# A decoder layer's sample attention: steps of four batches in place of steps of two

## The chip, the cores and the metric

The kernel runs on one core of one Trainium2 chip. Its time is the device time of one execution in microseconds (us); of several executions the median stands. The profile is one further execution, taken by the hardware profiler. In its rows PE is TensorE's matrix multiplication and PEld its loading of weights; DVE is VectorE, ACT is ScalarE, POOL is GpSimd and SP is SyncE, whose queue issues most of the transfers (SPq). A matrix product of f32 data appears as two records, so that a run of eight products is shown as x16.

## The reference, cut to what matters

One layer of a decoder is computed for two groups of requests that share the weights: a prompt of 1024 positions, and a sample group of 8 batches with 8 new positions each and 4096 cached ones. The change is in the attention of the sample group. It has 8 query heads of 64 channels in two groups of 4, and each group has one key and value head. Three branches are added with gates: the attention over compressed blocks of the cache, the attention over selected blocks of 64 cached positions, and a window of 512.

```python
def cmp_attention(q, k_cmp, v_cmp, q_pos):
    ...
    s = jnp.einsum('btgrd,bcgd->bgrtc', q, k_cmp).astype(jnp.float32) * ATTN_SCALE
    p = masked_softmax(s, mask)
    o = jnp.einsum('bgrtc,bcgd->btgrd', p.astype(v_cmp.dtype), v_cmp)
...
def slc_block_attention(q_b, idx_b, ok_b, pos_b, k_blocks, v_blocks):
    ...
    s = jnp.einsum('btgrd,bgtkpd->bgrtkp', q_b, k_sel).astype(jnp.float32) * ATTN_SCALE
    ...
    return jnp.einsum('bgrtkp,bgtkpd->btgrd', p.astype(v_sel.dtype), v_sel)
...
def window_sample(q, kw_ext, vw_ext, pos0):
    ...
    return window_attention(q[:, None], kw_ext[:, None], vw_ext[:, None], q_pos, k_pos)[:, 0]
```

Here b is the batch, t the position, g the group, r the head within the group, d the channel. A batch and a group have r x t = 4 x 8 = 32 query rows. The kernel doesn't gather the selected blocks: it computes the scores of all cached positions and masks those that were not selected.

## The kernel before, in words

The kernel is one Python class that writes the instructions of the whole layer. Its `run` is a planner: tasks are generators, and at each turn the one with the lowest priority number that is ready by the planner's clock goes on. The clock adds up costs written in the code (`mm`, `use`); for an f32 product with at most 64 weight columns `mm` counts 0.55 of the full cost, with at most 32 columns 0.27, and never fewer than 128 moving columns. The order in which the planner writes the instructions is the base of the order on each engine; a scheduler with a timeline of its own may still move them. `tc.issue_after(x)` makes the instructions written in its block come after x on x's engine.

After the input projection comes the stage with attention, in which three tasks share the engines. `prompt_attention` works through 32 units (8 query blocks, 2 halves of the heads, 2 branches), with priority 1.8 + `v_done`/32. `compress` makes the compressed keys and values of the sample batches 3 to 7 (0 to 2 are done earlier) from cache pages, which pass through three `stream` tiles. `sample_attention` has priority 2 + 1.1 x `u_done`/36. When the stage is over the kernel goes on to the output projection, whose weights and inputs are loaded by SP.

**The sample attention before.** The batches are taken in four pairs p; a pair has 9 units, 8 of 512 cached positions for each of the two batches and one for the window, 36 units in all. The queries stand in `qb` with 64 columns for a batch: 32 for each group, and zeros in the 64 channel rows of the other group. So the product of `qb` (128 rows, 64 columns) with the keys of 512 positions gives the 64 query rows of a batch, and the two batches of a pair fill the 128 partitions of a bank of PSUM, each in its own half of TensorE's columns. One unit is then:

1. two score products of 512 columns into a bank `S` (L135, `bank<-unit,qb` or `bank<-stream,qb`; the keys and values of a unit come in a tile `unit` or `stream`);
2. the mask and the row minimum on DVE (L1264, L1267), the exponential on ACT (L1271), both into `e`;
3. four transposes on PE (L139, `bank<-ident,e`) and the copy to `spt` (L150 on ACT or L152 on DVE);
4. eight value products of 128 columns (L135, `bank<-unit,spt` or `bank<-stream,spt`: 4 tiles of positions, 2 batches), each with both groups' values, of which a query row needs one half;
5. the copy of the sum to `part`.

A unit's tile is filled by 8 gathers of 128 KB from `cacheB` (L517) or by one load of the window (L1232). Two tiles `unit` are there from the start; the three `stream` tiles join once all batches are compressed (`cmp_done == 8`, in `sample_load`). A unit is written when the one before the last is done (`u_done >= u - 1`).

`sample_select` comes ahead of a pair. It waits for the pair's two compressed batches, computes the compressed branch (products named `bank<-kvc,qb` and `bank<-kvc,ct`), the new positions (`bank<-kn,qb`, `bank<-vt,ct`), the choice of blocks (`bias`) and the gates (`gr`). `sample_combine` joins the 12 parts of a pair on DVE (`co`, L1319 and L1321) and stores them to `mix_d` through SP (L1332), where the output projection reads them.

Other products that the text names: `bank<-wada,sc` (L135) has 32 weight columns and four column tiles side by side, `bank<-vt,c_w` has weights of 64 rows and 64 columns in four tiles, two row halves by two column halves; `bank<-pt,vt` are the value products of the prompt, and `bank<-kh,qs` its scores.

Of the kernel before, what the change touches and what calls it, by code (L numbers as in the profile page):

```python
# [17 lines left out]
P = 128  # L18
# [42 lines left out]
class Kernel:  # L61
# [181 lines left out]
    def constants3(self, c):  # L243
        nc = self.nc
        with self.pool("ctmp") as tp:
# [47 lines left out]
            a = tp.tile([P, 4, 64], F32, name="a")  # L293
            for b2 in range(2):
                nc.gpsimd.iota(a[64 * b2:64 * b2 + 64], pattern=[[-16, 4], [1, 64]], base=-8 * b2,
                               channel_multiplier=0, allow_small_or_imprecise_dtypes=True)
            ge = tp.tile([P, 4, 64], F32, name="ge")
            nc.vector.tensor_scalar(ge, a, 0.0, None, op0=OP.is_ge)
            ok = tp.tile([P, 4, 64], F32, name="ok")
            nc.vector.scalar_tensor_tensor(ok, a, tv[:, 0:1], ge, op0=OP.is_le, op1=OP.mult)  # L300
            self.m_new = c.tile([P, 4, 64], F32, name="m_new")
# [10 lines left out]
            self.sel = c.tile([P, 4, P], F32, name="sel")  # L312
            si = tp.tile([P, 4, 2, 8, 8], F32, name="si")
            for p in range(4):
                nc.gpsimd.iota(si[:, p], pattern=[[-8, 2], [0, 8], [-1, 8]], base=-64 - 16 * p,
                               channel_multiplier=1, allow_small_or_imprecise_dtypes=True)
            nc.vector.tensor_scalar(self.sel.rearrange("a p r -> a (p r)"), si.rearrange("a p b g t -> a (p b g t)"),
# [3 lines left out]
            hi = tp.tile([P, 8], F32, name="hi")  # L321
            for b2 in range(2):
                nc.gpsimd.iota(hi[64 * b2:64 * b2 + 64], pattern=[[-8, 8]], base=0, channel_multiplier=1,
                               allow_small_or_imprecise_dtypes=True)
            hg = tp.tile([P, 8], F32, name="hg")
            nc.vector.tensor_scalar(hg, hi, 0.0, None, op0=OP.is_ge)
            self.hind = c.tile([P, 8], F32, name="hind")
            nc.vector.scalar_tensor_tensor(self.hind, hi, 7.0, hg, op0=OP.is_le, op1=OP.mult)

# [773 lines left out]

    def sample_setup(self, pool):
        nc = self.nc
        self.qb = pool.tile([P, NB, 64], F32, name="qb")
        nc.vector.memset(self.qb, 0.0)
        for g in range(2):
            s = slice(64 * g, 64 * g + 64)
            nc.vector.tensor_copy(  # L1110
                self.qb[s].rearrange("p b (g r t) -> p g b r t", g=2, r=4)[:, g],
                self.q[s, :, SEQ:].rearrange("p r (b t) -> p b r t", t=NT))
        self.kn = pool.tile([P, 2, 64], F32, name="kn")
        nc.vector.tensor_copy(self.kn, self.ksw[:, :, SEQ:])
        self.use("dve", 1.5)

    def rows(self, b2):
        return slice(64 * b2, 64 * b2 + 64)

    def sample_select(self, pool, p, st):  # L1120

        nc = self.nc
        part = pool.tile([P, 12, P], F32, name="part", bufs=2)
        nm = pool.tile([P, 12], F32, name="nm", bufs=2)
        den = pool.tile([P, 12], F32, name="den", bufs=2)
        st.update(part=part, nm=nm, den=den)
        kv = []
        yield from self.hold(lambda: self.cmp_done >= 2 * p + 2)
        for b2 in range(2):
            t = pool.tile([P, 2, 256], F32, name="kvc", bufs=2)  # L1130
            nc.sync.dma_start(t, self.cmp_d[2 * p + b2])
            kv.append(t)
        yield self.use("dma", 1.5, self.t["pe"]) + 2.5
        S = yield from self.bank_of("S")
        S2 = yield from self.bank_of("S")
        for b2 in range(2):
            self.mm(S[self.rows(b2), 0:256], self.qb[:, 2 * p + b2], kv[b2][:, :, 0:P], True, True)
        for b2 in range(2):
            self.mm(S2[self.rows(b2), 0:128], self.qb[:, 2 * p + b2], self.kn.rearrange("p j t -> p (j t)"), True, True)

# [48 lines left out]
        for h in range(2):  # L1189
            self.tr(tr[:, h * P:(h + 1) * P], pc[:, 1 + h * P:1 + (h + 1) * P])  # L1190
# [985 lines left out]
```

## Time and profile before

| | |
|---|---|
| time, median of 3 runs (lowest to highest) | 1708.9 us (1705.45 to 1711.09) |
| time of the profiled execution | 1706.47 us |
| span of its records | 1704.6 us |
| PE busy | 1609.1 us, 94% of the span |
| DVE busy | 1113.6 us, 65% |
| ACT busy | 817.8 us, 48% |
| POOL busy | 706.9 us, 41% |
| granted TensorE clock over the span | 0.98 of full speed |

The time has 1.9 us outside the span. The busy time of PE counts the modelled ends of products that overlap in the array, so that 94% is not the share of the array's peak. Times in the rows below are counted from the start of the span.

### The profile page before, as it was taken

Reading aid. Unit: us, or ns where it says so; the run is one execution under the profiler, and the core shown is the slowest. Engines: PE = TensorE matmul, PEld = TensorE weight load, DVE = VectorE, ACT = ScalarE, POOL = GpSimd, SP = SyncE. Lnnn points to the kernel's source line nnn. Section 1 sums busy time; section 2 is a strip of 40 time slices with the busy share of each in tenths; the row PEclk is TensorE's granted clock in tenths of the full one; section 3 lists DMA queues with packets and bytes.
Section 4 is the critical chain, followed back from the end, with each engine's and each line's share of the span. In section 5 each row is a group of like instructions: output and inputs, shape, how many; then the busy total and the mean of one; then the engine's idle time right before and its main releaser. Section 6 shows DMA issues by size and latency. Waiting matters only on the chain. (4 is left out here: it accounts for less than half of the span.)

```text
span 1704.6 us, 34455 instructions
## 1 busy us (share of the span) xinstructions
PE 1609.1 (94%) x11961; PEld 1414.5 (83%) x11961; DVE 1113.6 (65%) x2830; ACT 817.8 (48%) x1878; POOL 706.9 (41%) x814
## 2 busy tenths in 40 slices
PE   6999999998998999999899789999999999889998
PEld 2999997887776566666699779999999998889997
DVE  4603326686665766866699986555555556988877
ACT  3512215245766776766675643332333334555554
POOL 3101110013331322222106476445555555898976
PEclk9899999998999999999999989999999999999999
DMA  9555564226654644432783223225222225744423
GB/s 341 170 179 177 162 208 143 80 63 196 196 171 125 199 138 146 143 92 83 233 244 90 92 72 117 96 97 191 97 100 96 96 97 187 240 128 132 131 82 122
DMA packets 177120, 245.08 MB, mean 144 GB/s; under 512 B 25889, under 2 KB 132578, under 8 KB 176626
## 3 DMA queue, kind: packets, MB, share of 16 engines
q1 hardware_dynamic: 157090, 215.37, 40.4%
q0 software_dynamic: 5840, 16.10, 2.9%
q10 hardware_dynamic: 14016, 11.41, 2.2%
q8 instruction: 95, 1.56, 0.4%
q14 instruction: 79, 0.65, 0.1%
HBM read 202.33 MB, written 44.67 MB: 145 GB/s over the span
## 5 line engine op out<-in xcount | busy, mean ns | idle before, releaser
L135 PE MATMUL bank<-b_hi,w_hi 128*128 128x272 f32 x1232 | 352.3, 292 | 9.2 <-DVE f_v L1551 4.5
L135 PE MATMUL bank<-b_lo,w_hi 128*128 128x272 f32 x1232 | 356.0, 291 | 2.9 <-DVE b_lo L160 2.9
L135 PE MATMUL bank<-b_hi,w_lo 128*128 128x272 f32 x1232 | 352.0, 290 | 1.3 <-DVE w_lo L160 1.3
L135 PEld LDWEIGHTS bank<-b_hi,w_hi 128*128 128x128 f32 x1232 | 232.3, 191 | 12.3 <-ACT b_hi L164 5.1
L135 PEld LDWEIGHTS bank<-b_lo,w_hi 128*128 128x128 f32 x1232 | 234.4, 190 | 4.5 <-DVE b_lo L160 4.4
L135 PEld LDWEIGHTS bank<-b_hi,w_lo 128*128 128x128 f32 x1232 | 233.1, 190 | 2.5 <-DVE w_lo L160 2.3
L160 POOL TENSOR_TENSOR w_s<-w_raw 128x512 f32<-128x512 f32 (+1 forms) x122 | 167.3, 1373 | 149.4 <-DVE w_lo L160 133.0
L1050 POOL TENSOR_SCALAR P<-P,st 128x128 f32<-128x128 f32 (+12 forms) x192 | 112.0, 592 | 259.2 <-DVE st L1048 86.3
L160 DVE TENSOR_TENSOR w_lo<-w_raw,w_hi 128x512 fp32r<-128x512 f32 (+2 forms) x129 | 115.0, 898 | 100.7 <-ACT w_hi L164 85.8
L164 ACT ACTIVATE w_hi<-w_raw 128x512 fp32r<-128x512 f32 (+2 forms) x130 | 86.4, 674 | 150.5 <-PE bank L135 100.5
L160 DVE TENSOR_TENSOR w_lo<-w_s,w_hi 128x512 fp32r<-128x512 f32 (+1 forms) x144 | 130.3, 908 | 43.1 <-ACT w_hi L164 39.2
L160 POOL TENSOR_TENSOR x<-x,d_m 128x272 f32<-128x272 f32 x144 | 140.1, 994 | 22.9 <-DVE x L1745 11.1
L135 PE MATMUL bank<-stream 128*128 128x128 f32 x1056 | 134.1, 285 | 6.8 <-DMA stream<-in_cacheA 6.7
L135 PEld LDWEIGHTS bank<-stream 128*128 128x128 f32 x1056 | 129.0, 200 | 13.8 <-issue 8.7
L164 ACT ACTIVATE w_hi<-w_s 128x512 fp32r<-128x512 f32 (+1 forms) x144 | 89.0, 624 | 102.4 <-PE bank L135 51.5
L135 PE MATMUL bank<-h_hi,w_hi 128*128 128x384 f32 (+1 forms) x384 | 130.9, 341 | 2.4 <-ACT py L865 2.3
L135 PE MATMUL bank<-h_hi,w_lo 128*128 128x384 f32 (+1 forms) x384 | 127.1, 331 | 0.0
L1042 ACT ACTIVATE P<-P,st 128x128 f32<-128x128 f32 (+12 forms) x192 | 113.2, 591 | 28.4 <-DVE st L1033 13.8
L135 PE MATMUL bank<-h_lo,w_hi 128*128 128x384 f32 (+1 forms) x384 | 126.6, 330 | 0.0
L135 PE MATMUL bank<-g_hi,w_hi 128*128 128x272 f32 x308 | 91.8, 300 | 14.5 <-DVE x L1745 8.2
L139 PEld LDWEIGHTS bank<-ident,P 128*128 128x128 f32 (+1 forms) x592 | 63.2, 138 | 50.7 <-issue 33.6
L1033 DVE CUSTOM_DVE_ANT_0 P<-bank,m_slc 128x256 f32<-128x256 f32 (+5 forms) x136 | 68.1, 513 | 54.2 <-PE bank L135 29.2
(368 smaller groups left out, 4114.8 us busy)
## 6 DMA issues: line engine op xcount, KB each, us to landing
wada<-in_wada SPq DMA_DIRECT2D x96, 256.0 KB, 5.3
stream<-in_cacheA SPq DMA_DIRECT2D x192, 128.0 KB, 3.3
w_raw<-in_wup SPq DMA_DIRECT2D x48, 512.0 KB, 4.3
unit<-in_cacheB SPq DMA_DIRECT2D x152, 128.0 KB, 2.3
g_raw<-g_d SPq DMA_DIRECT2D x70, 272.0 KB, 3.1
stream<-in_cacheB SPq DMA_DIRECT2D x104, 128.0 KB, 2.2
w_raw<-in_wout SPq DMA_DIRECT2D x24, 512.0 KB, 4.7
g_d<-f_T SPq DMA_DIRECT2D x84, 136.0 KB, 1.8
```

The source lines that it names most:

```text
L135: return self.nc.tensor.matmul(out, lhsT, rhs, start=start, stop=stop, skip_group_check=chain)
L139: self.nc.tensor.transpose(out, in_, self.ident)
L160: (self.nc.vector if eng == "dve" else self.nc.gpsimd).tensor_tensor(out, a, b, op=op)
L164: self.nc.scalar.activation(hi, src, AF.Copy)
L1033: nc.vector.tensor_tensor_reduce(out=Pt[:, h, col:col + n], in0=S[:, p0:p0 + n], in1=mk, scale=-1.0, scalar=3e38, op0=OP.add, op1=OP.min, ...
L1042: nc.scalar.activation(Ps, Ps, AF.Exp, scale=-1.0, bias=sy[:, 0:1], accum_out=sy[:, 1:2])
L1050: nc.gpsimd.tensor_scalar(Ps, Ps, sy[:, 3:4], 0.0, op0=OP.mult, op1=OP.add)
```

## The change

The 8 batches are taken in two groups Q of four. A query block of `qb` has 32 columns without zeros: the heads and positions of one group, its 64 channels in the group's own half of the rows. A step u (18 in all) holds two of the earlier units, thus four batches, and has two banks `S`, one for each group g, with the four batches in four strips of 32 partitions. Its eight score products have 64 rows, 32 weight columns and 512 moving columns, and each has a tile of the array of its own (2 row halves by 4 column strips). The 32 value products have 128 rows, 32 weight columns and 64 moving columns (2 groups, 4 tiles of positions, 4 batches). DVE, ACT and the transposes have as many instructions for a step as for two units before, except that the sum is copied once for a step. `together` writes the first product and puts the others behind it on PE; the first is one of the last batch's. The two buffers `e` and the two `spt` are now both taken by one step, as are two tiles `unit` or `stream`.

`sample_select` waits for four compressed batches, is spawned twice at the start, loads keys and values apart (four loads each) and goes through the two groups one after the other; a step starts when both are done. `sample_combine` runs twice; for the sum it has 48 DVE instructions of 64 columns in all, in place of 48 of 128.

```diff
     def sample_setup(self, pool):
         nc = self.nc
-        self.qb = pool.tile([P, NB, 64], F32, name="qb")
-        nc.vector.memset(self.qb, 0.0)
-        for g in range(2):
-            s = slice(64 * g, 64 * g + 64)
-            nc.vector.tensor_copy(
-                self.qb[s].rearrange("p b (g r t) -> p g b r t", g=2, r=4)[:, g],
-                self.q[s, :, SEQ:].rearrange("p r (b t) -> p b r t", t=NT))
+        self.qb = pool.tile([P, NB, 32], F32, name="qb")
+        nc.vector.tensor_copy(self.qb.rearrange("p b (r t) -> p b r t", r=4),
+                              self.q[:, :, SEQ:].rearrange("p r (b t) -> p b r t", t=NT))
...
+    def rows(self, b):
+        return slice(32 * b, 32 * b + 32)
+
+    def group(self, g):
+        return slice(64 * g, 64 * g + 64)
+
+    def together(self, products):
+
+        first = products[0]()
+        with self.tc.issue_after(first.ins):
+            for f in products[1:]:
+                f()
+
+    def sample_scores(self, S, col, Q, keys):
+
+        def score(b, g):
+            k = keys(b)[self.group(g)]
+            n = 1
+            for d in k.shape[1:]:
+                n *= d
+            return self.mm(S[g][self.rows(b), col:col + n], self.qb[self.group(g), 4 * Q + b], k, True, True)
+
+        tiles = [(b, g) for b in reversed(range(4)) for g in reversed(range(2))]
+        self.together([lambda v=v: score(*v) for v in tiles])
+
+    def sample_select(self, pool, Q, st):
...
+        yield from self.hold(lambda: self.cmp_done >= 4 * Q + 4)
+
+        def load(x):
+            t = [pool.tile([P, 2, P], F32, name="kvc", bufs=4) for b in range(4)]
+            for b in range(4):
+                nc.sync.dma_start(t[b], self.cmp_d[4 * Q + b][:, :, x * P:(x + 1) * P])
+            return t, self.use("dma", 1.5, self.t["pe"]) + 2.5
...
+        self.sample_scores(S, 0, Q, lambda b: K[b])
+        self.sample_scores(S, 256, Q, lambda b: self.kn)
+        V, at = load(1)
+        for g in range(2):
...
             for h in range(2):
                 n = P if h == 0 else NCMP - P
-                self.mm(o[r, 0:P], ct[:n, h, r], kv[b2][:n, h, P:2 * P], h == 0, h == 1)
...
+                for b in range(4):
+                    self.mm(o[self.rows(b), 0:64], ct[:n, h, self.rows(b)], V[b][:n, h, self.group(g)], h == 0, h == 1)
...
-        for u in range(36):
-            p, x = divmod(u, 9)
...
+        for Q in range(2):
+            self.spawn(1, self.sample_select(pool, Q, sts[Q]))
+        for u in range(18):
+            Q, x = divmod(u, 9)
+            st = sts[Q]
+            yield from self.hold(lambda: "at" in st and 2 * u + 1 in self.loads and self.u_done >= 2 * u - 2)
+            kv, at, src = zip(*[self.loads.pop(2 * u + c) for c in range(2)])
+            yield max(*at, st["at"])
+            S = []
+            for g in range(2):
+                S.append((yield from self.bank_of("S")))
+            self.sample_scores(S, 0, Q, lambda b: kv[b // 2][:, b % 2, :, 0:P])
...
+    def sample_values(self, pool, u, st, kv, es, nx, src):
...
         o = yield from self.bank_of("a")
-        for t in range(4):
-            for b2 in range(2):
-                self.mm(o[self.rows(b2), 0:P], pt[:, t * P + 64 * b2:t * P + 64 * b2 + 64], kv[:, b2, t, P:2 * P],
-                        t == 0, t == 3)
-        self.give("a", self.evac(st["part"][:, nx], o[:, 0:P], P))
-        self.unit_free.append(src)
+        self.together([lambda g=g, t=t, b=b: self.mm(
+            o[self.rows(b), self.group(g)], pts[g][:, t * P + 32 * b:t * P + 32 * b + 32],
+            kv[b // 2][:, b % 2, t, P + 64 * g:P + 64 * g + 64], t == 0, t == 3)
+            for g in reversed(range(2)) for t in range(4) for b in range(4)])
+        self.give("a", self.evac(st["part"][:, nx].rearrange("p g d -> p (g d)"), o[:, 0:P], P))
+        self.unit_free += src
         self.sample_load(pool)
-        self.u_done += 1
+        self.u_done += 2
```

The constants of the sample group (`m_new`, `sel`, `hind`, in `constants3`) follow the new order of rows: `sel` and `m_new` have half the columns, `hind` has one set for each group, and POOL writes their counters in 14 pieces in place of 8.

## Rows read from the trace of the kernel before

**Rows 1.** Attention stage: stretch, length, PE, PEld, DVE, ACT, POOL busy, clock, DMA, GB/s

```profile
400.00:560.00 160.00, 149.49 (x1162) 111.75 (x1162) 93.89 (x459) 109.15 (x297) 48.82 (x102) 0.99 0.56 170
560.00:600.00 40.00, 38.04 (x277) 23.30 (x275) 29.44 (x146) 28.96 (x81) 12.11 (x21) 1.00 0.65 192
600.00:800.00 200.00, 199.99 (x1499) 125.22 (x1497) 138.04 (x648) 132.59 (x336) 56.66 (x82) 1.00 0.42 124
800.00:840.00 40.00, 31.83 (x207) 20.03 (x204) 25.60 (x97) 28.02 (x65) 9.39 (x12) 0.92 0.56 175
```

**Rows 2.** PE's timeline at the stage's end: start, length, what, idle before

```profile
836.30 0.60 PE L135 MATMUL bank<-mh,w_hi 128*128 128x272 f32 x1 [5.35 <-ACT w_hi L164]
```

**Rows 3.** PE's groups by shape, 395 to 800: records | busy, mean ns | idle

```profile
L135 PE MATMUL bank<-unit,qb 128*64 128x512 f32 x80 | 24.3, 610 | 1.5 <-DMA unit<-in_cacheB 0.6 <-DVE pt L152 0.5 <-DVE qs L983 0.5
L135 PE MATMUL bank<-unit,spt 128*64 128x128 f32 x320 | 23.0, 280 | 0.0
...
L135 PE MATMUL bank<-stream,spt 128*64 128x128 f32 x256 | 18.1, 279 | 0.0
L135 PE MATMUL bank<-stream,qb 128*64 128x512 f32 x64 | 17.4, 604 | 1.2 <-DMA stream<-in_cacheB 1.2
...
L135 PE MATMUL bank<-vt__285,ct 64*64 64x128 f32 x32 | 2.6, 282 | 0.0
...
L135 PE MATMUL bank<-kn,qb 128*64 128x128 f32 x16 | 2.1, 288 | 0.0
```

**Rows 4.** instructions that touch `kvc` alone, by stretches

```profile
395.00:800.00 405.00, 5.90 (x48) 2.92 (x48) 1.00 0.50 150
```

**Rows 5.** instructions that touch `spt` alone, by stretches

```profile
600.00:800.00 200.00, 27.50 (x384) 20.88 (x384) 1.36 (x2) 12.33 (x21) 1.00 0.42 124
```

**Rows 6.** PE's timeline, a score run and a value run of a unit

```profile
761.01 1.03 PE L135 MATMUL bank<-unit,qb 128*64 128x512 f32 x4
761.97 0.66 PE L139 MATMUL bank<-ident,e 128*128 128x128 f32 x4
...
773.69 1.09 PE L135 MATMUL bank<-unit,spt 128*64 128x128 f32 x16
774.72 0.66 PE L139 MATMUL bank<-ident,e 128*128 128x128 f32 x4
```

**Rows 7.** PE's timeline, products in four tiles of 32 columns; then 258.36 to 258.39

```profile
258.37 1.07 PE L135 MATMUL bank<-wada,sc 128*32 128x256 f32 x16
259.37 0.41 PE L135 MATMUL bank<-h_hi,w_hi 128*128 128x320 f32 x1
...
258.37 0.42 PE L135 MATMUL bank<-wada,sc 128*32 128x256 f32 x4
```

**Rows 8.** PE's timeline, 64 moving columns in four tiles, to 303.735, 303.745 and 304.0

```profile
303.63 0.29 PE L135 MATMUL bank<-vt,c_w 64*64 64x64 f32 x4
...
303.63 0.33 PE L135 MATMUL bank<-vt,c_w 64*64 64x64 f32 x5
...
303.63 0.34 PE L135 MATMUL bank<-vt,c_w 64*64 64x64 f32 x8
303.91 0.41 PE L135 MATMUL bank<-h_hi,w_hi 128*128 128x320 f32 x1
```

**Rows 9.** the engines in the slice in which DVE is busiest

```profile
700.00:720.00 20.00, 20.00 (x150) 11.69 (x148) 17.97 (x73) 13.77 (x35) 5.51 (x9) 1.00 0.53 155
```

**Rows 10.** SP's timeline: first load of units; last store of the sample group

```profile
387.79 9.51 SPq L517 DMA_DIRECT2D unit<-in_cacheB  x16
...
787.14 0.38 SPq L1332 DMA_DIRECT2D mix_d<-smo  x1
```

**Rows 11.** transfers by line: queue, count, size, median us to landing

```profile
unit<-in_cacheB SPq DMA_DIRECT2D x152, 128.0 KB, 2.3
```

**Rows 12.** POOL's timeline, stores of the fourth and the eighth compressed batch

```profile
412.85 0.60 POOL L656 DMA_DIRECT2D cmp_d<-kvo  x1
...
558.67 0.59 POOL L656 DMA_DIRECT2D cmp_d<-kvo  x1 [1.33 <-DVE co L1321]
```

More of the change, by code (lines that the diff above doesn't have):

```diff
@@ L1212, in sample_select @@
-        nc.vector.tensor_copy(part[:, 8:11:2], o[:, 0:256].rearrange("p (h c) -> p h c", h=2))
-        self.give("t", self.use("dve", 0.35, self.t["pe"]))
+                for b in range(4):
+                    self.mm(o[self.rows(b), 0:64], ct[:n, h, self.rows(b)], V[b][:n, h, self.group(g)], h == 0, h == 1)
+            nc.scalar.activation(part[:, 11, g], o[:, 0:64], AF.Copy)
+            self.give("a", self.use("act", 0.2, self.t["pe"]))
+            o = yield from self.bank_of("t")
+            for j in range(2):
+                for b in range(4):
+                    self.mm(o[self.rows(b), 64 * j:64 * j + 64], ct[64:128, 2 + j, self.rows(b)],
+                            self.vt[64:128, 8, j * P + 64 * g:j * P + 64 * g + 64], True, True)
@@ L1243, in sample_attention @@
         self.sample_load(pool)
[L1244 to L1259 removed]
+        sts = [{} for _ in range(2)]
@@ new lines, in sample_attention @@
+        for Q in range(2):
+            self.spawn(1, self.sample_select(pool, Q, sts[Q]))
[5 more added lines that the diff above has]
+            yield max(*at, st["at"])
+            S = []
+            for g in range(2):
+                S.append((yield from self.bank_of("S")))
+            self.sample_scores(S, 0, Q, lambda b: kv[b // 2][:, b % 2, :, 0:P])
@@ L1269, in sample_attention @@
[L1269 to L1284 removed]
+            es = []
@@ new lines, in sample_attention @@
+            self.spawn(2, self.sample_values(pool, u, st, kv, es, nx, src))
+            yield 0.0
+    def sample_values(self, pool, u, st, kv, es, nx, src):
+        pts = []
+        for e, ready in es:
+            yield ready
+            tr = yield from self.bank_of("t")
+            for t in range(4):
+                self.tr(tr[:, t * P:(t + 1) * P], e[:, t * P:(t + 1) * P])
+            pt = pool.tile([P, 512], F32, name="spt", bufs=2)
+            r = self.evac(pt, tr, 512)
+            self.give("t", r)
+            pts.append(pt)
@@ new lines, in sample_combine @@
+        o = pool.tile([P, 2, 64], F32, name="co", bufs=2)
+        for g in range(2):
+            nc.vector.tensor_scalar(o[:, g], part[:, 11, g], gr[:, g, 0:1], None, op0=OP.mult)
+            for c in range(11):
+                nc.vector.scalar_tensor_tensor(o[:, g], part[:, c, g], w[:, g, c:c + 1], o[:, g], op0=OP.mult, op1=OP.add)
+        yield self.use("dve", 6.5, self.t["pe"]) + 0.5
+        tr = yield from self.bank_of("t")
+        self.tr(tr[:, 0:P], o.rearrange("p g d -> p (g d)"))
```

285 lines of the change are left out of this document (117 added, 168 removed).

## The prediction

> **What bounds the kernel now.** I read the page first: PE is busy for most of the span, no other engine comes near it. That is an average, so I cut the stage that the change touches into stretches [rows 1]. From 400 to 600 PE stands idle for 12.5 of 200 us; from 600 to 800 it has no gap at all, while DVE is busy for 138 and ACT for 133 us of the 200. So in the stage the sum of PE's work sets the pace, and of the rest nothing is even close in the mean; in its busiest slice DVE reaches 18 of 20 us [rows 9]. The reader should then look at who ends last. The last store of the sample group is issued at 787.1 [rows 10], and PE goes on with the prompt alone until 831.0, where it waits 5.35 us for the weights of the output projection [rows 2]. The sample group thus has 44 us of slack; what it takes from PE still delays the prompt, because both share PE. What is saved of PE's time there moves the end of the stage, and everything after it, forward. The wait for the weights stays: it starts when the stage ends.
>
> **What the score and value products cost now.** The 36 units have 144 score records, busy 24.3 + 17.4 = 41.7 us, and 576 value records, busy 23.0 + 18.1 = 41.1 us [rows 3]. Busy time overlaps what follows: a score run of 1.03 us is followed after 0.96, a value run of 1.09 after 1.03 [rows 6]. Less 0.07 and 0.06 for each of 36 runs this is 39.2 + 38.9 = 78.1 us of PE's time.
>
> **What they cost after.** A run of eight products with 32 weight columns and 256 moving ones, four side by side, takes 1.00 us to the next start, and four records start within 0.03 us [rows 7]. Each column strip has 4 records of 256 columns there, 1024 columns in sequence. A run of eight records of 64 moving columns in four tiles, 128 columns in sequence, takes 0.28 us [rows 8]. The two give (1.00 - 0.28)/896 = 0.80 ns for a column and 0.18 us for a run, whatever its length. Rows 8 also show tiles of two row halves side by side: four records, two in each half, before the fifth.
>
> A step's score run has eight tiles side by side, 2 records of 512 columns each: as long as today's run of two tiles, 0.96, and six more starts under 0.01 each, so 1.00 us for four batches. That eight tiles stream together is shown by no row; rows 7 and 8 show four column strips, and two halves of each kind, and I take their product. If the row halves went one after the other it would be 4 records of 512 columns, 1.82 us. A step's value run has 16 rounds of four records of 64 columns, again 1024 columns in sequence: 1.03 us, as rows 6. 18 steps cost 18 x (1.00 + 1.03) = 36.5 us, and 41.6 us of PE's time go.
>
> The unknown of this sum is a round of 64 columns. Rows 8 show it from both sides: the fifth record starts 0.11 us after the first, with the first loading of weights inside, and the slope gives 0.05. If every round took 0.11, the value run would be 16 x 0.11 + 0.18 = 1.94 us. I take 0.05: in rows 6 a record pair of 128 columns goes by in 1.03/8 = 0.13 us with all overhead in it, so the length still counts there.
>
> The Trainium skill speaks against this edit: "TensorEngine Tiling (Array Packing)", Instruction Overhead, says that a matmul has an overhead of some 60 cycles, so that a dimension which is already small should not be divided further, and the page on "TensorE: Matmul & The Clock Gate" (Wait — 56ns, not 53.3ns?) has a floor of about 25 ns between starts. The value products are cut from 128 to 64 columns, just at that size, and are twice as many for a batch. By that floor the 64 records of a step would take an estimated 1.6 us and the gain on values would be a quarter of mine. The trace does not agree for tiles side by side: four starts in 0.03 us [rows 7]; it has no such run of 64 records.
>
> **The other parts.** The selection's products are busy 5.9 + 2.1 + 2.6 = 10.6 us now [rows 3, 4], 9.6 less the ends of 16 runs. After, for each Q, the compressed scores are 2 records of 256 columns in sequence (0.59 us), the new positions 2 of 128 (0.38), and for each group the two value runs 4 of 64 (0.38 each): 2.5 us, 5.0 for both Q. 4.6 us go. Transposes, `rsum` and `sel` products keep their number. DVE and ACT keep the instructions of score, exponential and transposed copy; half of the copies of the sum go, and the sum over parts is narrower. All this lies beside PE and is counted as nothing; without that cover it would be a gain too. The constants and `qb` cost DVE less ahead of the stage and POOL six more small counters: a microsecond either way, taken as 0.
>
> Together 46 us of PE's time go.
>
> **How much of it the clock sees.** The value records lie for 27.5 of 41.1 us, 67%, between 600 and 800 [rows 3, 5], so 31 us of the 46 leave the stretch without gaps. With 169 us there DVE would be busy for 82% and ACT for 78%. In the slice of rows 9 only 2 us can go before DVE is the bound, so I take 26 of 31, between the bounds 31 and 15. The other 15 us leave the stretch in which PE already waits for 12.5; I take 7, between 0 and 15. Sum: 33 us.
>
> What stands against it there: the step waits for two tiles. Until all batches are compressed at 558.7 [rows 12] only two are there, so a step holds both and the next load starts when it is done. That load is 16 gathers, 9.5 us of issue on SP [rows 10] and 2.3 to land [rows 11]; behind them on SP wait the pages for `compress`. The selection waits for the fourth batch, stored at 412.9, where the third was enough before. Neither is PE's time: the prompt fills it, as long as it has work, and the 44 us of slack take up the delay of the sample group.
>
> **The sum.** 1706.5 - 33 = 1673.5 us for the profiled execution. The runs' median lies 2.4 us above it, so 1676 us.
>
> **Rivals.**
> - *PE saves as forecast* (62%): 1676 us, its own range 1663 to 1690.
> - *Short records don't shrink* (14%): a round of 64 columns takes 0.11 us. The value runs cost 18 x 1.94 = 34.9, the selection 16 rounds x 0.06 = 1 us more; 46 becomes 46 - 16.4 - 1 = 29 us, at the same share of 0.72 it is 21: 1688 us. For it: the 0.11 of rows 8. Against it: the first loading stands inside. The floor that the skill's page gives would lead to about this time.
> - *Another engine takes over* (14%): PE's savings turn into waits for DVE and ACT. Nothing of the first 15 and half of the 31 us: 1694 us. For it: rows 9 and the idle time before 600. Two things in the code add to it: a step holds two of the four banks `S`, and both `e` and both `spt`, so that two steps overlap less. Against it: 65% DVE and 68% ACT over 400 to 800.
> - *The sample group falls behind and ends last* (7%): while it has two tiles, a step takes 11.8 us for its load, and as no load runs ahead, the step's own chain on top. Between a first step at some 445 and 559 this allows six or so of 18. If the steps left over run alone after the prompt, each costs its chain of an estimated 6 us rather than 3.8 of PE, and the last store on SP, with the loads of the output projection behind it, is late. It decides from about six steps left over (6 x 6 against 33): with eight it is 48 - 33 = 15 us slower, 1724 us. Against it: the slack of 44 us.
> - *No change* (3%): the runs are broken up by the scheduler, so that tiles no longer stream together and the gain is lost: 1709 us.
>
> **How the numbers follow.** The predicted time is that of the first. A change under 0.3% (5 us) is about what measurements of this kernel can't tell from none. Faster: 62 + 14 + 11 of the 14 = 87%. Same: 3 + 3 = 6%. Slower: 7%. The range goes from 1660 (all 46 us, and a little for DVE's lighter work) to 1702, which takes in the second and third rivals; what is left out is the slower one, no change and a still larger gain.
>
> **What would show it.** Score runs of 16 records and value runs of 64 in the changed trace: each should be followed after about 1.0 us; 1.8 for scores means that the row halves take turns, 1.9 for values that short records don't shrink. The wait for the output weights, now at 831, should come some 33 us earlier, with PE still busy for over 95% between 600 and its end. The last store of the sample group should still be ahead of the prompt's end. If PE has more than 20 us of new gaps in the stage, behind DVE or ACT, the share of 0.72 was wrong; if the gaps stand behind gathers of `unit`, the two tiles were.

## The result, and the profile after

The change makes the kernel slower: 1720.5 us (median of 4, 1713.5 to 1723.0) against 1708.2, a ratio of 1.0071 with a 95% interval of 1.0052 to 1.0090. The forecast was 1676. The profiled execution is the lowest of the four, 1713.5 us with a span of 1711.7, so that the two traces differ by 7.1 us where the medians differ by 12.3.

First the products themselves. PE's timeline of the changed kernel shows a score run and a value run that nothing disturbs, as [rows 6] did before:

```profile
757.91 1.09 PE L135 MATMUL bank<-stream,qb 64*32 64x512 f32 x16
758.93 0.51 PE L135 MATMUL bank<-kh,qs 128*128 128x512 f32 x1
...
735.34 1.10 PE L135 MATMUL bank<-stream,spt 128*32 128x64 f32 x64
736.37 0.50 PE L135 MATMUL bank<-kh,qs 128*128 128x512 f32 x1
```

Eight score tiles are followed after 1.02 us (forecast 1.00) and 64 value records after 1.03 us (forecast 1.03). Tiles of both row halves and all four column strips do stream side by side, and a round of 64 columns does take 0.05 us. PE's groups by shape, from 395 to 800, answer to [rows 3]: the busy time of the values fell from 41.1 to 27.7 us, that of the scores rose from 41.7 to 43.2 (part of it at half clock, see the account below), and both score groups have idle time ahead of them that ends with a gather's landing (9.2 and 4.1 us; before 1.2 and 0.6).

```profile
L135 PE MATMUL bank<-unit,qb 64*32 64x512 f32 x144 | 21.7, 704 | 6.1 <-DMA unit<-in_cacheB 4.1 <-DVE st L1044 1.0 <-DVE st L1048 0.5
L135 PE MATMUL bank<-stream,qb 64*32 64x512 f32 x144 | 21.5, 626 | 9.2 <-DMA stream<-in_cacheB 9.2
L135 PE MATMUL bank<-unit,spt 128*32 128x64 f32 x576 | 13.9, 221 | 0.5 <-DVE st L1048 0.5
L135 PE MATMUL bank<-stream,spt 128*32 128x64 f32 x576 | 13.8, 221 | 0.0
```

Now the stage, cut alike in both kernels (stretch, length, busy time of PE, PEld, DVE, ACT and POOL, granted clock, DMA share, GB/s). The kernel before:

```profile
350.00:470.00 120.00, 110.11 (x812) 93.46 (x811) 82.11 (x330) 71.97 (x193) 36.35 (x87) 0.94 0.55 165
470.00:600.00 130.00, 120.10 (x904) 82.37 (x904) 82.43 (x384) 91.56 (x243) 38.75 (x74) 1.00 0.54 163
600.00:780.00 180.00, 180.00 (x1367) 112.61 (x1363) 124.36 (x587) 120.34 (x306) 47.85 (x71) 1.00 0.40 120
```

The changed kernel:

```profile
350.00:470.00 120.00, 100.73 (x773) 88.02 (x772) 77.08 (x309) 64.32 (x175) 34.56 (x90) 0.89 0.48 140
470.00:600.00 130.00, 121.09 (x1129) 84.87 (x1130) 77.66 (x372) 90.03 (x238) 40.06 (x75) 0.92 0.48 144
600.00:780.00 180.00, 164.25 (x1912) 100.56 (x1910) 120.85 (x566) 108.80 (x277) 46.23 (x68) 0.96 0.51 151
```

Two columns matter, PE's busy time and the clock. From 600 to 780 PE had no gap; now it has 15.8 us of them. And the clock, which stood at its upper level (1.00, that is 2.4 GHz) from 470 to 780, is granted at half (1.2 GHz) for a part of every stretch. What a stretch loses can be read from a row: its idle time, plus (1 - clock) x length (a little too much, as idle time at half clock stands in both terms). That is 17.1, 9.9 and 0.0 us before, 32.5, 19.3 and 23.0 us after: 27 against 75.

What ends PE's gaps from 600 to 780 is in its waits (us in total, times, longest):

```profile
PE bank L135 <- DMA stream<-in_cacheB: 9.2, 6, 2.3
PE bank L135 <- DMA unit<-in_cacheB: 4.1, 2, 3.5
PE bank L135 <- ACT pt L150: 0.9, 1, 0.9
PE bank L135 <- DVE pt L152: 0.8, 1, 0.8
```

13.3 of the 15.8 us are score products that wait for their gathers. The longest one, on PE and on SP's queue, between 680 and 711:

```profile
698.17 1.26 PE L135 MATMUL bank<-stream,qb 64*32 64x512 f32 x8
699.37 0.65 PE L135 MATMUL bank<-pt,vt__285 128*64 128x256 f32 x4
...
700.54 1.06 PE L135 MATMUL bank<-stream,qb 64*32 64x512 f32 x6
701.52 0.65 PE L135 MATMUL bank<-pt,vt__285 128*64 128x256 f32 x4
...
702.69 1.04 PE L135 MATMUL bank<-stream,qb 64*32 64x512 f32 x2
...
704.84 0.65 PE L135 MATMUL bank<-pt,vt__285 128*64 128x256 f32 x4
708.97 1.42 PE L135 MATMUL bank<-unit,qb 64*32 64x512 f32 x16 [3.48 <-DMA unit<-in_cacheB]
710.32 0.63 PE L135 MATMUL bank<-kh,qs 128*128 128x320 f32 x1
710.75 0.47 PE L135 MATMUL bank<-kl,qs 128*128 128x320 f32 x1
```

```profile
680.43 15.23 SPq L517 DMA_DIRECT2D stream<-in_cacheB  x24
696.26 10.50 SPq L517 DMA_DIRECT2D unit<-in_cacheB  x16
```

Three things are to be seen. The 16 gathers of the step take SP 10.5 us, to 706.8, and the last lands 2.2 us later; PE reached the score product at 705.5. PE works in order, so the prompt's products behind it stand too. And after the wait the clock is low: the prompt's product of 320 columns at 710.32 is followed after 0.43 us, where the same product is followed after 0.23 at full clock (at 793 to 820). Above it, the step before was taken apart by products of the prompt, in 8, 6 and 2 records, and each part is followed after about 1 us (1.20, 0.98, 0.98): 3.2 us in place of 1.02. The score runs of the 18 steps came as 24.

No tile was missing in this wait: from 680.4 to 706.8 SP issued the gathers of five tiles one after the other and waited 0.8 us in all. In the wait before 660.31 it was a tile. SP could issue the gathers of the step's second tile only when the value products at 652.00 had freed it, and PE stood for 2.3 us until they had landed:

```profile
652.00 1.10 PE L135 MATMUL bank<-stream,spt 128*32 128x64 f32 x64
653.13 10.33 SPq L517 DMA_DIRECT2D stream<-in_cacheB  x16
660.31 1.39 PE L135 MATMUL bank<-stream,qb 64*32 64x512 f32 x16 [2.29 <-DMA stream<-in_cacheB]
```

The timelines of PE, SP and POOL answer to three more groups: the stage's end, [rows 2], came 11.3 us later; the last store of the sample group, [rows 10], 4 us earlier; the eighth compressed batch, [rows 12], 5 us earlier.

```profile
847.60 0.59 PE L135 MATMUL bank<-mh,w_hi 128*128 128x272 f32 x1 [2.45 <-ACT w_hi L164]
```

```profile
783.05 0.37 SPq L1358 DMA_DIRECT2D mix_d<-smo  x1
```

```profile
553.77 0.60 POOL L656 DMA_DIRECT2D cmp_d<-kvo  x1 [4.04 <-DVE kvo L651]
```

**The account of the stage.** From 350 to the first product of the output projection the time is split by the records: from a product's start to the next one's is work, less what PE stands idle; work at half clock counts half as work and half as clock.

| us | before | after | difference |
|---|---|---|---|
| products at full clock | 452.3 | 420.8 | -31.5 |
| of these scores | 37.8 | 27.3 | -10.5 |
| of these values | 36.3 | 19.8 | -16.5 |
| of these selection | 13.6 | 9.1 | -4.5 |
| lost to half clock | 6.0 | 27.6 | +21.6 |
| PE idle | 28.0 | 49.4 | +21.4 |

The row of the selection has its transposes and its `rsum` and `sel` products in it. The sum is +11.5, and the stage ends 11.3 us later. What follows after it is 4.2 us shorter (864.1 against 868.3 us to the end). The account explains the 7.1 us between the two traces, not all of the 12.3 between the medians.

Gathers alone don't make the idle time. In PE's waits from 395 to 850 those for gathers of the sample group rose from 1.8 to 13.3 us, and those for DVE and ACT, without the weights of the output projection (`w_hi`), from 10.1 to 16.9. The largest of the latter before, and the largest two after:

```profile
PE bank L139 <- DVE pt L152: 2.6, 3, 1.4
```

```profile
PE bank L135 <- DVE m L1179: 2.7, 1, 2.7
PE bank L135 <- DVE pt L152: 2.7, 3, 1.3
```

### The profile page after: what moved, and what is told of

It reads as the page before. It is cut to its first block, busy times and chain, and to the rows that moved or that the text cites. A ratio compares the mean times of both kernels' runs of the same rounds, so it can differ in the third digit from the quotient of the medians.

```text
span 1711.7 us, 36017 instructions
## 1 busy us (share of the span) xinstructions
PE 1598.5 (93%) x12775; PEld 1406.1 (82%) x12775; DVE 1099.9 (64%) x2818; ACT 807.3 (47%) x1845; POOL 708.8 (41%) x820
## 4 chain that ended last, share of the span: by engine, by line
PE 61%; DVE 15%; DMA 7%; issue 6%; POOL 4%; ACT 4%; SPq 3%; ACTq 0%; POOLq 0%; DVEq 0%
PE bank L135 56%; PE bank L139 4%; SPq L517 3%; DVE w_lo L160 2%; DMA w_raw<-in_wup 2%; POOL w_s L160 2%; POOL x L160 1%; DVE b_lo L160 1%; DVE P L1033 1%; DVE x L1770 1%; DMA w_raw<-in_wdown 1%; DMA stream<-in_cacheB 1%; DVE g_lo L160 1%; DVE d_lo L160 1%; ACT w_hi L164 1%
## 5 line engine op out<-in xcount | busy, mean ns | idle before, releaser
L1050 POOL TENSOR_SCALAR P<-P,st 128x640 f32<-128x640 f32 (+13 forms) x192 | 113.7, 602 | 272.6 <-DVE st L1048 104.5
L160 DVE TENSOR_TENSOR w_lo<-w_s,w_hi 128x512 fp32r<-128x512 f32 (+1 forms) x144 | 126.8, 884 | 45.0 <-ACT w_hi L164 40.8
L135 PEld LDWEIGHTS bank<-stream 128*128 128x128 f32 x1056 | 130.3, 202 | 10.3 <-issue 5.5
L1042 ACT ACTIVATE P<-P,st 128x640 f32<-128x640 f32 (+12 forms) x192 | 113.0, 590 | 27.8 <-DVE st L1038 13.9
L135 PE MATMUL bank<-g_hi,w_hi 128*128 128x272 f32 x308 | 91.6, 300 | 15.7 <-DVE x L1770 7.2
L139 PE MATMUL bank<-ident,P 128*128 128x128 f32 (+1 forms) x592 | 99.3, 290 | 6.1 <-POOL P L1050 2.3
```

The source lines that it names most:

```text
L135: return self.nc.tensor.matmul(out, lhsT, rhs, start=start, stop=stop, skip_group_check=chain)
L139: self.nc.tensor.transpose(out, in_, self.ident)
L160: (self.nc.vector if eng == "dve" else self.nc.gpsimd).tensor_tensor(out, a, b, op=op)
L1042: nc.scalar.activation(Ps, Ps, AF.Exp, scale=-1.0, bias=sy[:, 0:1], accum_out=sy[:, 1:2])
L1050: nc.gpsimd.tensor_scalar(Ps, Ps, sy[:, 3:4], 0.0, op0=OP.mult, op1=OP.add)
```

## The experiments

The theories. **A**: a step needs two of five tiles, the second is loaded too late, PE waits in order and the clock falls. **A2**: not the tiles are at fault but the planner's numbers, which place the score products too early. **B**: holding two banks and both `e` makes the gaps. **C**: the binding behind the first product does. **D**: a second loss comes from the selection, which waits for four batches. A ratio is to the kernel before, in runs on the same chip.

| run | time, us | ratio, 95% interval | lost 350-470 | 470-600 | 600-780 |
|---|---|---|---|---|---|
| before | | 1 | 17.1 | 9.9 | 0.0 |
| the change | 1720.5 | 1.0071, 1.0052 to 1.0090 | 32.5 | 19.3 | 23.0 |
| noload | 1685.6 | 0.9885, 0.9854 to 0.9916 | 33.3 | 9.8 | 5.1 |
| before_noload | 1699.9 | 0.9976, 0.9960 to 0.9992 | 16.5 | 5.9 | 0.0 |
| six | 1699.8 | 0.9962, 0.9940 to 0.9985 | 21.7 | 27.8 | 13.8 |
| before_tiles3 | 1711.8 | 1.0032, 1.0019 to 1.0045 | 14.3 | 14.6 | 0.9 |
| loose | 1714.2 | 1.0056, 1.0041 to 1.0072 | 32.3 | 18.2 | 21.6 |
| costs | 1712.8 | 1.0046, 1.0031 to 1.0061 | 32.3 | 22.5 | 20.1 |
| late | 1695.5 | 0.9925, 0.9901 to 0.9948 | 32.9 | 15.7 | 12.7 |
| late7 | 1723.4 | 1.0097, 1.0063 to 1.0131 | 32.2 | 17.6 | 15.5 |
| costs_late | 1708.2 | 1.0015, 1.0001 to 1.0028 | 33.8 | 20.1 | 18.1 |
| before_late | 1692.8 | 0.9925, 0.9901 to 0.9948 | 15.1 | 8.3 | 0.0 |
| costs_early4 | 1708.5 | 1.0012, 0.9996 to 1.0028 | 19.5 | 36.4 | 28.6 |
| noload_early4 | 1674.4 | 0.9825, 0.9805 to 0.9845 | 18.3 | 7.7 | 2.9 |
| before_noload_early4 | 1694.0 | 0.9934, 0.9911 to 0.9958 | 24.4 | 1.4 | 0.0 |
| before_wait4 | 1714.7 | 1.0050, 1.0033 to 1.0067 | 23.6 | 10.3 | 0.2 |
| before_noload_wait4 | 1703.4 | 0.9982, 0.9970 to 0.9993 | 25.7 | 1.7 | 0.2 |
| pair | 1699.8 | 0.9954, 0.9930 to 0.9979 | 15.9 | 8.4 | 0.1 |
| pair_late | 1686.1 | 0.9889, 0.9858 to 0.9920 | 15.8 | 8.0 | 0.1 |
| pair_costs_late | 1684.4 | 0.9891, 0.9871 to 0.9910 | 17.8 | 4.5 | 0.0 |

The last three columns are idle time plus (1 - clock) x length from rows like those above, of the one profiled execution of each run. That of costs_early4 was the slowest of its ten (1718.1 us), that of late7 the slowest of its four (1726.6). Gains and losses in the text go by the ratios, of 1707 us.

**Without loads: noload and before_noload.** A freed tile goes back with its contents, and only the first five loads are made:

```diff
             src = self.unit_free.pop(0)
+            if not isinstance(src, str):
+                self.loads[self.unit_next] = (src[1], self.t["pe"], src)
+                self.unit_next += 1
+                continue
```

> The changed kernel, but only the first load of each of the five tiles is made; the later 31 of the 36 loads are left out and a tile's old contents are used again. Theory A (a step needs two of five tiles, its second load comes too late, PE stands in order at the score products and the clock falls after it): the 13.3 us of waits for gathers vanish, idle time of PE in the stage falls from 49 to about 30 us, the stretches at half clock from 62 to some 25 us, and the time falls by 30 us or more, to 1680 to 1692. Rival B (larger steps with both banks and both e held by one step are what leaves gaps): the waits move to other releasers and the time stays above 1710. Rival C (issue as one run upsets the order): above 1710 too.

> The kernel before with the same loads left out, as the control for noload. Its PE waits only 2.7 us for gathers of the sample group in the stage, so theory A expects 1700 to 1708, hardly less than 1708. If it gains as much as noload does, loads cost both kernels the same and theory A falls.

noload, in the view of the stretches:

```profile
350.00:470.00 120.00, 99.91 (x786) 86.27 (x784) 78.08 (x321) 66.52 (x178) 34.48 (x90) 0.89 0.47 140
470.00:600.00 130.00, 121.50 (x1374) 85.61 (x1374) 84.75 (x400) 98.44 (x270) 41.76 (x80) 0.99 0.31 93
600.00:780.00 180.00, 176.65 (x1856) 109.96 (x1856) 118.69 (x599) 128.51 (x313) 56.50 (x80) 0.99 0.09 26
```

By the ratios the loads cost the changed kernel 31.8 us (1.0071 - 0.9885, of 1707) and the kernel before 4.1. The gaps and the low clock vanish together, where the loads were: 9.5 us between 470 and 600, 17.9 after 600. Between 350 and 470 nothing changes. The waits for gathers vanish, as forecast, but PE's idle time falls to 40.8 us and not to 30, and its time at half clock to 39 us and not to 25. The 31.8 us are not a clean price: to the planner a tile that isn't loaded again is ready at once, so that the edit also gives another order, and a new order alone was worth 13 us (before_late, below). B and C are out as the main cause, since banks, `e` and binding are as before the edit. But B isn't gone: without loads the waits for DVE and ACT from 395 to 850, `w_hi` left out, are 18.7 us, against 8.7 in the control. The loss of the first stretch remains for D.

**The binding: loose.**

```diff
-        first = products[0]()
-        with self.tc.issue_after(first.ins):
-            for f in products[1:]:
-                f()
+        for f in products:
+            f()
```

> The changed kernel without the binding of a step's products behind their first one. Theory A: the waits for gathers stay, so does the time, 1715 to 1725. Rival C (the binding upsets the order or breaks runs up): the time falls to 1700 or less. If the binding does what it says, runs are broken up more than now and the time rises above 1725.

1714.2 us, in none of the three ranges but nearest to theory A's: the waits for gathers are there (14.2 us in the stage), and the score runs came as 24 again. That is 2.6 us less than the change, and the two intervals overlap. So the binding's cost isn't clear of noise, and it keeps little together; other products still come between.

**The number of tiles: before_tiles3 and six.** In before_tiles3 `self.unit_free += ["stream"] * 3` has 1 in place of 3. In six the tile `unit` has three buffers; `ksq`, `ko` and `kvo` of `compress` take the places of `pre` and `vt`, and `mo`, `smo`, `co` and `sn` have one buffer each.

> The kernel before, but only one of the three stream tiles joins the sample group, three tiles in place of five: two units in flight and one load ahead, the same proportion as the changed kernel has with five tiles for steps of two. Theory A: PE's waits for gathers rise from 2.7 to 8 us or more and half clock with them, 1712 to 1730. If loads of gathers are hidden anyway with three tiles, 1706 to 1710, and theory A must find another place.

> The changed kernel with all its loads, and a sixth tile (three unit in place of two; room for it from small buffers that share or lose their second copy), so that two steps in flight leave two tiles to load ahead, a whole step's. Theory A (too few tiles for steps of two): the waits for gathers fall under 5 us, the loss between 600 and the sample group's end from 23 to under 8 us, and the time falls by 12 to 25 us, to 1695 to 1708. If the number of tiles isn't it, 1715 to 1725.

six falls by 19 us (1.0071 to 0.9962), and its loss after 600 from 23.0 to 13.8 us, the gathers' share from 13.3 to 4.3 us:

```profile
PE bank L135 <- DMA stream<-in_cacheB: 4.3, 2, 2.7
PE bank L135 <- DVE co L1351: 3.0, 1, 3.0
```

The time is the one that was forecast, but the two signs of the theory were missed. In the stretch before, where the changed kernel doesn't wait for gathers of the sample group, six waits 5.6 us for them (all of `unit`), so that its waits for gathers in the stage fall only to 9.9 us and not under 5; the loss there rises from 19.3 to 27.8 us, and after 600 it isn't under 8. Ahead of 470 the loss falls by 10.8 us, with another order through the shared buffers. So how much of the 19 us is the tile's stays open. before_tiles3 speaks against a theory of tiles alone: with three tiles the kernel before waits 2.9 us for gathers, hardly more than the 1.8 with five (the view has 1.8, not the 2.7 of the expectation), and loses 5 us by another way: its score runs, of which two units often shared one, came as 49 in place of 34 and took 7.5 us more. A unit there needs one tile only, and the load of the next goes on beside it.

**The planner's numbers: costs, late, late7, costs_late, before_late.** costs counts a bound run at 0.55 of the sum of its products; the others add 4 or 7 us to the landing of a tile that the planner expects:

```diff
+        pe = self.t["pe"]
         first = products[0]()
...
+        self.t["pe"] = pe + 0.55 * (self.t["pe"] - pe)
...
-                at = self.gather(kv[:, 4 * b2:4 * b2 + 4], "cacheB", 4 * Q + 2 * c + b2, 4 * x, 4)
+                at = self.gather(kv[:, 4 * b2:4 * b2 + 4], "cacheB", 4 * Q + 2 * c + b2, 4 * x, 4) + 4.0
```

> The changed kernel, with the planner's clock told what a run of eight score or 32 value products takes (0.55 of what it counts now, 1.0 in place of 1.84 us). Theory A2 (the planner counts 3.7 us of PE for a step's products where the trace has 2.05, so its clock runs ahead of PE and writes the score products before their tile has landed): waits for gathers fall from 13.3 to under 8 us and the time falls by 5 to 20 us, to 1700 to 1715. If the order matters less than the number of tiles, 1718 to 1722 as before the edit.

> The changed kernel, with the planner told that a tile's gathers land 4 us later than it counts now; nothing else. Theory A2 (it is the place in PE's order that is wrong, PE reaches the score products some us before the second tile has landed): waits for gathers fall from 13.3 to under 5 us, half-clock time falls, 1695 to 1710. If the tiles themselves are too few, the steps start later and the prompt runs alone for longer at the end: 1710 to 1725.

> Run late with 7 us in place of 4. Theory A2: what was left of the waits for gathers in late (5.3 us in two waits) goes, and the time stays at 1690 to 1698; that an arbitrary order was lucky at 4 us would let it come back to 1710 or more. If tiles are too few, the steps come later still and the prompt stands alone at the end, 1700 to 1710.

> Both corrections together: a step's products counted at 0.55, and gathers landing 4 us later. If they are two parts of one fault (the planner's clock ahead of PE and of the loads), 1690 to 1697, no better than late alone; if they are two faults, 8 us less than late, 1684 to 1690.

> The control for run late: the kernel before, with the planner told the same, that a tile's gathers land 4 us later. Theory A2 (the planner's place for the score products was wrong only for steps of two tiles; before, three tiles were loaded ahead): within 0.3% of the kernel before, 1701 to 1712. If any new order of the stage is worth ten us, it falls by as much as late did, to 1695, and late shows no cause.

late gave 25 us, its waits for gathers fell to 6.2 us and the loss to half clock to 13.3: it seemed a proof of A2. Its control took that away, for before_late gained 13 us with the same number, where PE hardly waits for gathers. With the same number in both, the change costs nothing and gains nothing (0.9925 and 0.9925). late7 waits 6.7 us for gathers, about as little as late, and still loses 25.9 us to half clock, and 17 us of its time lie behind the stage (881.4 us from there to the end, against 864.1 in the changed kernel); no run shows why. Both corrections together gave less than late alone. So A2 falls as the cause. What the five runs show is a spread: the changed kernel and its four nudged orders lie between 1695 and 1723 us, the kernel before and its one at 1707 and 1693. costs kept the score runs whole (18 runs, 20.2 us at full clock) and gained 4 us, though its waits for gathers are 14.8 us. In the whole table one thing doesn't move: every kernel with steps of four loses 12.7 us or more after 600 with its loads, every kernel with steps of two 0.9 or less. Of A, then, the loads are shown; that they are late by the planner's fault is not.

**The selection: costs_early4, noload_early4, before_noload_early4, before_wait4, before_noload_wait4.** The first three have `EARLY = 4` (four batches compressed ahead of the stage) in place of 3. The last two make the selection by pairs wait as the changed one does, one after the other (`selected` counts those that are done):

```diff
-        yield from self.hold(lambda: self.cmp_done >= 2 * p + 2)
+        yield from self.hold(lambda: self.cmp_done >= 4 * (p // 2) + 4 and self.selected == p)
```

> The kernel of run costs, and four batches compressed ahead of the stage rather than three, so that the first selection finds its four batches at the start of the stage. Theory D (a second loss: until the fourth batch is there and both groups are selected, to 464, PE has too little to do, 13 us idle and 14 us at half clock between 395 and 464): the first step starts before 440 and the time falls by 5 to 12 us against costs, to 1701 to 1708. Rival: compressing earlier only moves the work ahead of the stage, 1713.

> Run noload (31 of 36 loads of the sample group left out), and four batches compressed ahead of the stage in place of three. Theory D (the first selection needs four batches and comes 36 us later, in which PE lacks work): the loss between 350 and 470 falls from 28 to about 15 us, and nothing takes its place since there are no loads: the time falls by 10 to 15 us against noload's 1686, to 1671 to 1676. If compressing earlier costs as much as it saves, 1682 to 1690.

> The control for noload_early4: the kernel before with the same loads left out and four batches compressed ahead. Its first selection needs two batches only, so theory D expects no gain against before_noload: 1695 to 1705. If it gains 10 us as well, the early compression is worth that to any kernel and says nothing of the selection.

> The kernel before; its selections wait for four compressed batches (the first two pairs) or all eight (the last two), as the changed kernel's do, one after the other; all else as it was. Theory D (the later selection leaves PE without work): the first score product comes 13 us later or more, after 440, the loss between 350 and 470 rises from 16 to 22 us or more, and the time by 5 to 12 us, to 1711 to 1718. If the selection's place isn't what counts, 1702 to 1709.

> Run before_noload with the same wait for four batches. Theory D: 5 to 12 us above before_noload, 1705 to 1712; otherwise 1697 to 1703.

The loss ahead of 470 follows the selection: 32.3 to 19.5 us and 33.3 to 18.3 with the fourth batch early, 17.1 to 23.6 and 16.5 to 25.7 with the wait put into the kernel before. Its row in before_wait4:

```profile
350.00:470.00 120.00, 104.81 (x745) 89.86 (x744) 79.60 (x335) 71.38 (x196) 36.89 (x91) 0.93 0.44 131
```

One run doesn't fit: the control before_noload_early4 loses 24.4 us there, more than the 16.5 of before_noload, and the sample group's first score product came later, at 454.3. But with the fourth batch early the prompt's first score product comes at 405 to 407, and at 387 to 390 otherwise, so that the stretch doesn't hold the same work. Over the whole stage, from 350 to its end, PE's idle time and half clock together fall by 17.1 us with the early batch in noload (52.3 to 35.2) and stay in its control (31.2 to 31.9); the wait adds 11.1 us to the kernel before and 9.3 to before_noload. In before_wait4 the sample group's first score product came at 430.4, not after 440 as expected (427.0 before, 464.2 in the changed kernel; 448.3 in costs_early4, where 440 was forecast), so the loss doesn't need a late start of the steps.

How much of it reaches the end is less clear: before_wait4 is 8.5 us slower, before_noload_wait4 1 us, where 5 to 12 were expected; noload gained 10 us from the early batch, its control 7. costs_early4 gained 5.8 us on costs (1.0046 to 1.0012), within the 5 to 12 of the forecast; its row with large losses after 470 is that of its slowest execution. That the later selection costs PE time in the stage is shown; what it costs at the end is between 1 and 9 us.

With both causes away, noload_early4 is at 1674.4 us, about the 1676 of the forecast. But like must be set against like: its control is at 0.9934, so the change itself is worth 0.9825/0.9934, 1.1% or 19 us, not 33, and each of the two is one order.

**The same idea with one tile for a unit: pair, pair_late, pair_costs_late.** The 36 units of two batches stay, without zeros: four strips (batch by group) in one bank; the selection and the combination use the same strips.

```diff
-            for b2 in range(2):
-                self.mm(S[self.rows(b2), 0:512], self.qb[:, 2 * p + b2], kv[:, b2, :, 0:P], True, True)
+            for b2, g, r, c in self.strips():
+                self.mm(S[r, 0:512], self.qb[c, 2 * p + b2], kv[c, b2, :, 0:P], True, True)
```

> Only one part of the change: the 36 units of two batches stay, each with one tile, one bank and one e, and the selection by pairs stays, but the queries have no zeros: four score products with 64 rows and 32 columns and 16 value products with 32 columns and 64 moving columns for a unit, without binding. A score run has 2 records of 512 columns in sequence as before (0.98 us), a value run 8 rounds of 64 (0.18 + 0.41 = 0.59 in place of 1.03 us): 36 x 0.44 = 16 us of PE's time go. Theory A (it is the two tiles of a step, loaded too late, that cost the time): with one tile for a unit the waits for gathers stay under 5 us and most of the 16 us are seen, 1690 to 1698. If narrow products by themselves upset the stage, 1708 or more.

> Run pair with the 4 us of run late. In pair PE waits 1.2 us for gathers of the sample group, so theory A2 expects no gain: 1694 to 1704.

> Run pair_late with the planner's floor for 32-column products lowered from 128 to 80 columns, which brings its count of a value run from 0.92 to 0.58 us. If counting closer to the trace helps, 1680 to 1685; by what costs did to late, worse, 1688 to 1700.

A value run of 32 records is followed after 0.585 us, as worked out (0.59), the values fall from 36.3 to 22.6 us, PE waits 2.0 us for gathers, and from 600 to 780 it is idle for 0.1 us. But pair gained 8 us, not most of the 16, and at 1699.8 us missed its 1690 to 1698: the score runs came as 39 in place of 34 and took 6.4 us more (44.2 against 37.8). pair_late beats pair by 11 us against expectation, as before_late did its kernel; like for like (0.9889/0.9925) the narrow products are worth 6 us there. pair_costs_late is no better than pair_late. Its stretches:

```profile
350.00:470.00 120.00, 106.96 (x909) 90.84 (x908) 84.05 (x354) 73.60 (x204) 38.99 (x96) 0.96 0.53 161
470.00:600.00 130.00, 125.52 (x1179) 84.53 (x1181) 88.74 (x413) 95.07 (x248) 41.78 (x76) 1.00 0.55 164
600.00:780.00 180.00, 180.00 (x1930) 107.32 (x1929) 125.15 (x599) 118.05 (x303) 50.22 (x72) 1.00 0.42 123
```

At 1684.4 us (0.9891 of the kernel before in the same runs; 0.9891/1.0071 = 0.982 of the changed one) it is, with pair_late, the best version with all its work that was run. The added 4 us alone gave the kernel before 13 of these 19 us.

## Why the prediction was wrong

- **The price of the new runs** was right: 1.02 and 1.03 us measured for 1.00 and 1.03. The rivals of short records that don't shrink and of row halves that take turns are out. The Trainium skill's rule against dividing a small dimension further ("TensorEngine Tiling (Array Packing)", Instruction Overhead) and its floor of about 25 ns between starts ("TensorE: Matmul & The Clock Gate", Wait — 56ns, not 53.3ns?) don't agree with this trace: 64 value records in 1.03 us are 16 ns each, in four tiles side by side. The forecast misread what the floor would do: 18 runs of 1.6 us would leave 10 of its 20.4 us on values, half and not a quarter.
- **The sum of PE's work** was too large: 31.5 us went at full clock, not 46. The values (16.5) and the selection (4.5) gave 21 of the forecast's 25. The score term was mis-sized: 18 x 1.00 was forecast, 27.3 us at full clock came. The runs were broken up (24 of them), and a part of a broken run costs about as much as the whole; and runs that follow a wait for gathers took 1.2 to 1.35 us. The scores of the kernel before took 37.8 us, near the 39.2 of the forecast. The rival of no change named the broken runs and was given 3%.
- **The step that failed** is "Neither is PE's time: the prompt fills it, as long as it has work." The load of two tiles and the wait for the fourth batch were both seen, and put down to the sample group's slack. But a score product that stands in PE's queue ahead of its gather holds the prompt behind it. In PE's place 23.0 us were lost after 600 (17.9 of them go without the loads), 9.4 more than before between 470 and 600, and 15.4 more ahead of 470, where the selection waits. The slack was there, 62 us from 783 to 845, and of no use. That the kernel then ends 12 us above the one before, and not level with it, can't be told from the order that the planner happened to write: four other orders of the changed kernel lie at 0.9925 to 1.0097.
- **The clock** was not in the sum at all. Half of what was lost, 21.6 of 43 us, is work at 1.2 GHz after gaps. The share of 0.72 for the 46 us was meant for waits behind DVE and ACT. From 600 to 780, where most of the saving was to leave, those hardly came (1.7 of 15.8 us of gaps in the rows of waits above), with DVE at 67%, so the third rival failed there. Over the stage they rose by 6.8 us, mostly ahead of 600, and not because DVE or ACT was full: from 350 to 600 DVE was busy for 60 to 64% and ACT for 54 to 69% of the two stretches.
- **The slower rival** has a number close to the result (1724 us) by luck, for its mechanism is wrong: the sample group didn't end last; the prompt did, at 845. By 559 three steps had started, not six, and the other fifteen still started by 758.

## What to carry to other kernels

A step that is made larger on an engine with the queue in order needs its operands ahead: count the tiles in flight and the loads ahead for the new step, not for the engine's share, and charge a late operand to everything that is queued behind it. Price gaps on TensorE above their length where the profile shows the clock fall after them; by how much isn't fixed (below). And where an order is planned by a list of costs, run the same nudge on the kernel before: an accidental order was worth 13 us here, more than the change, and a control without the edit is what tells the two apart.

## What the runs showed of the hardware

- Eight tiles of 64 rows and 32 columns ran in 1.02 us, as long as two tiles of 128 rows and 64 columns before (0.86 to 1.01).
- 64 records of 64 columns in four strips took 1.03 us, 32 took 0.585: 14 ns for each further record.
- The granted clock fell in the stage of every kernel, but the 0.5 level held for 62 us after and 16 us before in the stage, with 49 and 28 us of gaps. There the added gaps of some tenths to 3.5 us cost as much again through the clock as by themselves (21.6 and 21.4 us). That isn't a fixed price: with 60.7 us of gaps the run costs lost 17.8 us to half clock, with 46.7 the run late7 lost 25.9, so that against the kernel before each us of added gaps came with 0.4 to 1.1 us.
